# The last normalisation of a diffusion layer: all sums but one tile's by the scalar engine, roots in pairs by GpSimd, both row operations by the vector engine

## The chip, the cores and the metric

The kernel runs on one core of one Trainium2 chip. The metric is the device time of one execution in microseconds (us); of several runs the median counts. The core's engines are TensorE (PE in the profile's rows; PEld are its weight loads), VectorE (DVE), ScalarE (ACT), GpSimd (POOL) and SyncE (SP), which here issues most of the DMAs. Each engine works through its own instructions in order, and semaphores order the engines among each other.

## The reference, cut to what matters

The layer mixes 2048 tokens of 1024 features by neighbourhood attention and a bidirectional mLSTM, sends them through a two-level mixture of experts, and closes with a layer norm. The change touches that last line alone:

```python
def _layer_norm(x, gain=None, bias=None):
    x32 = x.astype(jnp.float32)
    mu = jnp.mean(x32, axis=-1, keepdims=True)
    var = jnp.mean(jnp.square(x32 - mu), axis=-1, keepdims=True)
    y = (x32 - mu) * lax.rsqrt(var + LN_EPS)
    if gain is not None:
        y = y * gain.astype(jnp.float32) + bias.astype(jnp.float32)
    return y.astype(x.dtype)
...
        x_next = _layer_norm(DEEPNORM_ALPHA * x_mid + g2 * moe, ln2_g[l], ln2_b[l])
```

All values are float32. The sum `DEEPNORM_ALPHA * x_mid + g2 * moe` is in the DRAM tensor `acc_d` when the last stage begins: the expert loop adds its outputs there by scattering DMAs.

## The kernel before, in words

The program runs its stages one after the other: modulation, input projection, attention and mLSTM, output projection and first norm, routing, then a loop over expert blocks (L1991 on), whose matmuls read weights that SyncE loads ahead, and whose results GpSimd scatters into `acc_d` (L2048). At the loop's end all engines meet. What follows is the last normalisation (L2094 to L2152), the only part that the change touches.

The 2048 rows are 16 tiles of 128 rows x 1024 columns (0.5 MB each), every one with a buffer of its own (`yy`, 16 buffers), so no load waits for a buffer. SyncE issues the loads of all tiles in order; between them stand two loads of the gain row (after tile 1) and the bias row (after tile 3), spread over 128 partitions (L2105, L2107). A tile goes through four steps: `moments`, `scales`, `gain`, `shifted`. The loop at the end issues `moments` of tile t, `scales` of tile t - 1, `gain` of t - 2 and `shifted` of t - 3 in one turn, and `in_order` keeps each engine's instructions in just the order in which the code names them, so this loop sets the order of every engine's queue.

Which engine does a step is a letter for each tile in the string `WAY`, "ADBADBCDCDBADBAD":

- The sums. In ways B and D (10 tiles) ScalarE makes two passes over the tile, a Copy scaled by -1/1024 whose accumulator gives minus the mean (L2116) and a Square with that as bias whose accumulator gives the sum of squared differences (L2117); the passes' own output goes to a tile `junk` that nobody reads. In A and C (6 tiles) VectorE makes two statistics and an aggregate (L2121, L2122). Two numbers per row result, in the small tile `mvf`.
- The roots. GpSimd makes variance + eps (L2127) and the power -1/2 (L2128) of one column, into `rsf`.
- The row operations. In A and D (10 tiles) VectorE does both, in place: (y - mean) * gain (L2137) and y * root + bias (L2144). In B and C (6 tiles) GpSimd makes a third small number, mean times root (L2131), ScalarE normalises the tile (L2132), GpSimd multiplies by the gain (L2139) and VectorE adds the bias (L2146).

SyncE writes each finished tile to the output (L2147), in the order of tiles.

Of the kernel before, what the change touches and what calls it, by code (L numbers as in the profile page):

```python
# [11 lines left out]
F32 = mybir.dt.float32  # L12
# [4 lines left out]
AF = mybir.ActivationFunctionType  # L17
OP = mybir.AluOpType
# [4 lines left out]
P = 128  # L23
D = 1024
# [4 lines left out]
EPS = 1e-5  # L29
# [6 lines left out]
def tile_layer(ctx, tc, A, out):  # L36
    nc = tc.nc

    def in_order(i):
        return tc.keep_in_program_order(i)  # L40
# [6 lines left out]
    nh = const.tile([P, 4], F32, name="nh")  # L47
# [24 lines left out]
    C = [None, None]  # L72
# [16 lines left out]
    st, ml = {}, {}  # L89
# [22 lines left out]
    with ExitStack() as es, ExitStack() as zes:  # L112
        xg = es.enter_context(tc.tile_pool(name="ip_xg", bufs=1, reuse_waits="tile"))
        ep = es.enter_context(tc.tile_pool(name="ip_e", bufs=4, reuse_waits="tile"))
        cp = es.enter_context(tc.tile_pool(name="ip_c", bufs=1, reuse_waits="tile"))
# [379 lines left out]
        for half in range(2):  # L495
# [94 lines left out]
            for qk in range(2):  # L590
# [5 lines left out]
                for h in range(4):  # L596
# [3 lines left out]
                    for g, n, t0 in groups:  # L600
# [20 lines left out]
                        if gate_rows_:  # L621
                            f, a = gate_rows_.pop(0)
# [261 lines left out]
    junk = []  # L884
# [23 lines left out]
    with ExitStack() as es:  # L908
        kpB = es.enter_context(tc.tile_pool(name="na_kB", bufs=1, reuse_waits="tile"))
        kps.append(kpB)  # L910
        sp = es.enter_context(tc.tile_pool(name="na_s", bufs=3, reuse_waits="tile"))
# [4 lines left out]
        sbs, pTs, pos_, rss, outs = {}, {}, {}, {}, {}  # L916
# [202 lines left out]
    with ExitStack() as es:  # L1119
        cc = es.enter_context(tc.tile_pool(name="op_cc", bufs=2, reuse_waits="tile"))  # L1120
        xn = es.enter_context(tc.tile_pool(name="op_n", bufs=3, reuse_waits="tile"))
        sp = es.enter_context(tc.tile_pool(name="op_s", bufs=4, reuse_waits="tile"))
        cp = es.enter_context(tc.tile_pool(name="op_c", bufs=1, reuse_waits="tile"))
# [608 lines left out]
    with ExitStack() as es:  # L1732
        sp = es.enter_context(tc.tile_pool(name="ro_s", bufs=1, reuse_waits="tile"))
# [4 lines left out]
        for l, G, c0 in ((0, 2, 0), (1, 4, 512)):  # L1738
            n = P // G
# [209 lines left out]
    with ExitStack() as es:  # L1949
        sp = es.enter_context(tc.tile_pool(name="mo_s", bufs=1, reuse_waits="tile"))  # L1950
# [143 lines left out]
    with ExitStack() as es:  # L2094
        cp = es.enter_context(tc.tile_pool(name="fi_c", bufs=1, reuse_waits="tile"))
        yp = es.enter_context(tc.tile_pool(name="fi_y", bufs=16, reuse_waits="tile"))
        sp = es.enter_context(tc.tile_pool(name="fi_s", bufs=4, reuse_waits="tile"))
        nh = cp.tile([P, 1], F32, name="nh2")
        in_order(nc.gpsimd.memset(nh[:], -0.5))
        ln2 = [cp.tile([P, D], F32, name=f"ln2{i}") for i in range(2)]  # L2100
        junk = cp.tile([P, D], F32, name="junk")
        ys, ms, rss = [], {}, {}
        for t in range(16):
            ys.append(yp.tile([P, D], F32, name="yy"))
            in_order(nc.sync.dma_start(ys[t][:], acc_d[t * P : (t + 1) * P, :]))  # L2105
            if t in (1, 3):
                in_order(nc.sync.dma_start(ln2[t // 2][:], A[("ln2_g", "ln2_b")[t // 2]].to_broadcast([P, D])))  # L2107


        WAY = "ADBADBCDCDBADBAD"  # L2110

        def moments(t):
            a = ys[t]
            mv = ms[t] = sp.tile([P, 2], F32, name="mvf")
            if WAY[t] in "BD":
                in_order(nc.scalar.activation(junk[:], a[:], AF.Copy, scale=-1.0 / D, accum_out=mv[:, 0:1]))  # L2116
                in_order(nc.scalar.activation(junk[:], a[:], AF.Square, bias=mv[:, 0:1], accum_out=mv[:, 1:2]))  # L2117
            else:
                st = sp.tile([P, 2, 6], F32, name="stf")
                for hh in range(2):  # L2120
                    in_order(nc.vector.bn_stats(st[:, hh, :], a[:, hh * 512 : (hh + 1) * 512]))  # L2121
                in_order(nc.vector.bn_aggr(mv[:], st[:]))  # L2122

        def scales(t):
            mv = ms[t]
            rs = rss[t] = sp.tile([P, 2], F32, name="rsf")
            in_order(nc.gpsimd.tensor_scalar(rs[:, 0:1], mv[:, 1:2], 1.0 / D if WAY[t] in "BD" else 1.0, EPS, OP.mult, OP.add))  # L2127
            in_order(nc.gpsimd.tensor_tensor(rs[:, 0:1], rs[:, 0:1], nh[:], OP.pow))  # L2128
            if WAY[t] in "AD":
                return  # L2130
            in_order(nc.gpsimd.tensor_scalar(rs[:, 1:2], mv[:, 0:1], rs[:, 0:1], -1.0 if WAY[t] == "C" else 1.0, OP.mult, OP.mult))  # L2131
            in_order(nc.scalar.activation(ys[t][:], ys[t][:], AF.Identity, bias=rs[:, 1:2], scale=rs[:, 0:1]))  # L2132

        def gain(t):
            y = ys[t][:]
            if WAY[t] in "AD":
                in_order(nc.vector.scalar_tensor_tensor(y, y, ms[t][:, 0:1], ln2[0][:], OP.add if WAY[t] == "D" else OP.subtract, OP.mult))  # L2137
            else:
                in_order(nc.gpsimd.tensor_tensor(y, y, ln2[0][:], OP.mult))  # L2139

        def shifted(t):
            y = ys[t][:]
            if WAY[t] in "AD":
                in_order(nc.vector.scalar_tensor_tensor(y, y, rss[t][:, 0:1], ln2[1][:], OP.mult, OP.add))  # L2144
            else:
                in_order(nc.vector.tensor_tensor(y, y, ln2[1][:], OP.add))  # L2146
            in_order(nc.sync.dma_start(out[0, t * P : (t + 1) * P, :], y))  # L2147

        for t in range(16 + 4):
            for f, n in ((moments, t), (scales, t - 1), (gain, t - 2), (shifted, t - 3)):  # L2150
                if 0 <= n < 16:
                    f(n)  # L2152


def consts():
# [62 lines left out]
```

## Time and profile before

| what | value |
|---|---|
| median of 3 runs | 2741.04 us (2736.18 to 2742.62) |
| the profiled execution's own time | 2737.7 us |
| its span, first to last record | 2735.9 us |
| busy share of the span: TensorE, VectorE, ScalarE, GpSimd | 91%, 46%, 29%, 29% |
| last normalisation, first load's issue to the span's end | 2667.30 to 2735.9 us |

The profile is one execution, with all times in us from the span's start. Durations in "mean ns" are nanoseconds. A busy share is an average over stages of different kinds; the change lies in the last 69 us, so the views below are of that stretch. An engine's row in a timeline shows its start, its duration, the instruction, and in brackets how long the engine had been idle before and who ended that. Where a row has "x2", two instructions of one kind that follow each other are merged and the duration is of both. A name such as `yy` stands for all buffers of that name.

### The profile page before, as it was taken

To read this page: it belongs to the slowest core of one execution; us is meant where nothing else is said; L and a number is where in the kernel's file an instruction comes from. 1 tells how busy PE (TensorE), PEld (TensorE's weight loads), DVE (VectorE), ACT (ScalarE), POOL (GpSimd) and SP (SyncE) were. 2 spreads that over 40 slices of the span, in tenths; PEclk is the share of its full clock that TensorE was granted. 3 is DMA by queue.
4 is the path that set the end of the run, shared out by engine and by line. 5 is a ranking of instruction groups with operands and counts; after the bars stand their busy time and mean duration, and the time that the engine had idled before them with its cause. 6 is when DMAs were issued, how large, how long until landed. Compare 5 with 4: busy or idle time off the path is not lost. (4 is left out here: it accounts for less than half of the span.)

```text
span 2735.9 us, 51840 instructions
## 1 busy us (share of the span) xinstructions
PE 2478.8 (91%) x17292; PEld 1567.5 (57%) x17292; DVE 1263.4 (46%) x2891; ACT 799.4 (29%) x1693; POOL 784.5 (29%) x912
## 2 busy tenths in 40 slices
PE   8999999999996899988999589978999999989880
PEld 4778667877886778876887433333333333333330
DVE  5546324357236976656578932222222222222225
ACT  4423115243234666656565410000000000000004
POOL 1212211002034535546434422211222222222127
PEclk9999999999999999999999789989999999999995
DMA  8634762434359979894654689999598897998916
GB/s 267 178 100 133 253 215 89 148 98 153 105 152 252 264 196 216 209 221 134 166 162 135 231 320 369 368 382 346 154 313 308 312 314 235 365 319 312 391 20 261
DMA packets 286892, 626.99 MB, mean 229 GB/s; under 512 B 79448, under 2 KB 142924, under 8 KB 262444
## 3 DMA queue, kind: packets, MB, share of 16 engines
q1 hardware_dynamic: 254716, 564.87, 62.0%
q0 software_dynamic: 31696, 60.09, 9.5%
q8 instruction: 71, 1.16, 0.2%
q10 hardware_dynamic: 352, 0.39, 0.1%
q14 instruction: 57, 0.47, 0.1%
HBM read 947.01 MB, written 97.42 MB: 382 GB/s over the span
## 5 line engine op out<-in xcount | busy, mean ns | idle before, releaser
L2048 POOL DMA_INDIRECT acc_d<-y,ids x112 | 174.4, 1557 | 739.3 <-DMA acc_d<-y,ids 266.4
L2011 DVE TENSOR_TENSOR sg<-sg,ph 128x128 f32<-128x128 f32 x112 | 39.8, 355 | 441.5 <-ACT sg L2010 441.5
L2010 ACT ACTIVATE sg<-ph 128x128 f32<-128x128 f32 x112 | 37.1, 331 | 697.8 <-PE ph L2005 498.1
L2005 PE MATMUL ph<-qkk,xT 128*64 128x512 f32 (+1 forms) x1344 | 234.0, 525 | 3.1 <-DMA qkk<-in_w_dram 3.1
L2005 PE MATMUL ph<-mask,xT 128*64 128x512 f32 x896 | 211.6, 615 | 24.8 <-DMA mask<-in_w_dram 24.8
L246 PE MATMUL ps<-xhi,whi 128*128 128x512 f32 (+1 forms) x576 | 221.6, 386 | 1.6 <-DVE ev L509 1.6
L248 PE MATMUL ps<-xhi,wlo 128*128 128x512 f32 (+1 forms) x576 | 220.2, 382 | 0.5 <-DVE wlo L235 0.5
L247 PE MATMUL ps<-xlo,whi 128*128 128x512 f32 (+1 forms) x576 | 220.3, 382 | 0.0
L2037 PE MATMUL py<-mo,gT 128*64 128x512 f32 x672 | 165.4, 628 | 24.2 <-DMA mask<-in_w_dram 13.2
L255 PE MATMUL ps<-whi,xhi 128*128 128x512 f32 x416 | 166.1, 401 | 1.3 <-ACT whi L234 1.3
L256 PE MATMUL ps<-wlo,xhi 128*128 128x512 f32 x416 | 164.3, 396 | 3.3 <-DVE wlo L235 3.3
L257 PE MATMUL ps<-whi,xlo 128*128 128x512 f32 x416 | 164.8, 397 | 0.0
L960 DVE CUSTOM_DVE_ANT_0 sb<-ps,bias 128x640 f32<-128x640 f32 (+1 forms) x128 | 113.9, 890 | 101.7 <-PE ps L957 78.3
L2005 PEld LDWEIGHTS ph<-mask,xT 128*64 128x64 f32 x896 | 62.1, 140 | 148.0 <-issue 148.0
L2005 PEld LDWEIGHTS ph<-qkk,xT 128*64 128x64 f32 (+1 forms) x1344 | 74.8, 128 | 114.9 <-issue 99.2
L2021 DVE COPY gT<-pg 128x128 f32<-128x128 f32 x112 | 40.2, 359 | 215.4 <-PE pg L2019 215.4
L1972 DVE TENSOR_SCALAR xT<-pxt,mod 128x96 f32<-128x96 f32 x456 | 135.0, 369 | 2.4 <-PE pxt L1965 2.4
L246 PEld LDWEIGHTS ps<-xhi,whi 128*128 128x128 f32 x576 | 108.4, 188 | 28.3 <-issue 3.2
L2045 DVE SCALAR_TENSOR_TENSOR y<-py,wgt,g2r 128x256 f32<-128x256 f32 x112 | 68.7, 613 | 119.5 <-PE py L2037 119.5
L968 ACT ACTIVATE sb<-sb,nm 128x640 f32<-128x640 f32 (+1 forms) x128 | 113.2, 884 | 33.0 <-DVE nm L960 28.8
L2010 ACT ACT_TABLE_LOAD x28 | 35.9, 1283 | 295.0 <-PE ph L2005 295.0
L248 PEld LDWEIGHTS ps<-xhi,wlo 128*128 128x128 f32 x576 | 108.4, 188 | 23.6 <-DVE wlo L235 0.9
(553 smaller groups left out, 5096.2 us busy)
## 6 DMA issues: line engine op xcount, KB each, us to landing
w<-in_w_dram SPq DMA_DIRECT2D x203, 1024.0 KB, 7.6
mask<-in_w_dram SPq DMA_DIRECT2D x114, 1024.0 KB, 8.7
qkk<-in_w_dram SPq DMA_DIRECT2D x114, 1024.0 KB
mo<-in_w_dram SPq DMA_DIRECT2D x171, 512.0 KB, 4.2
bias<-in_w_dram SPq DMA_DIRECT2D x58, 1024.0 KB
xo<-in_w_dram SPq DMA_DIRECT2D x115, 512.0 KB, 9.3
bias<-in_w_dram SPq DMA_DIRECT2D x58, 512.0 KB
qkk<-in_w_dram SPq DMA_DIRECT2D x58, 512.0 KB
```

The costliest lines, as they stand in the source:

```text
L246: nc.tensor.matmul(ps, wh_, xhi[g, k][:], start=k == 0, stop=False)
L247: nc.tensor.matmul(ps, wh_, xlo[g, k][:], start=False, stop=False)
L248: nc.tensor.matmul(ps, wl_, xhi[g, k][:], start=False, stop=k == KC - 1)
L255: nc.tensor.matmul(ps, xh, his[k], start=k == 0, stop=False)
L256: nc.tensor.matmul(ps, xh, los[k], start=False, stop=False)
L257: nc.tensor.matmul(ps, xl, his[k], start=False, stop=k == KC - 1)
L960: in_order(nc.vector.tensor_tensor_reduce(out=sb[:, 0:L], in0=ps[:, off:768], in1=bt[:, 0:L], scale=-0.125, scalar=3.0e38, op0=OP.add, op1 ...
L968: in_order(nc.scalar.activation(sb[:, 0:L], sb[:, 0:L], AF.Exp, bias=nm[:], scale=-1.0, accum_out=rss[n // 8][:, n % 8 : n % 8 + 1]))
L1972: i = nc.vector.tensor_scalar(xT[u][:, k], pxt[:, k, 0:96], mod2[:, 1, k : k + 1], mod2[:, 0, k : k + 1], OP.mult, OP.add)
L2005: in_order(nc.tensor.matmul(ph[j * n : (j + 1) * n], xT[u][:, k, t0 : t0 + n], w13[k][:, :, j * NH : (j + 1) * NH], start=k == 0, stop=k = ...
L2037: in_order(nc.tensor.matmul(py[j * n : (j + 1) * n, :], gT[:, b_, j_ * n : (j_ + 1) * n], w2t[c][:, j * NY : (j + 1) * NY], start=c == 0, ...
L2048: sc = nc.gpsimd.indirect_dma_start(out=acc_d[:].rearrange("t (g n) -> (t g) n", g=G), out_offset=bass.IndirectOffsetOnAxis(ap=ids[u][:, l ...
```

## The change

The table of ways goes. Tile 0 keeps its statistics on VectorE; the sums of the other 15 tiles are ScalarE's two passes. The sums and roots stand in small tiles of two columns, one for each of the pairs (1, 2), (3, 4) to (13, 14), and of one column for tiles 0 and 15; GpSimd makes eps and power for both tiles of a pair in one instruction each, when the second tile's sums are there. Both row operations of all 16 tiles are VectorE's. The gain row is loaded after tile 0 and the bias row after tile 1. All sums and roots are issued first, and then the row operations, the gain of tile t with the shift of tile t - 2.

```diff
@@ -2094,62 +2094,64 @@
     with ExitStack() as es:
         cp = es.enter_context(tc.tile_pool(name="fi_c", bufs=1, reuse_waits="tile"))
         yp = es.enter_context(tc.tile_pool(name="fi_y", bufs=16, reuse_waits="tile"))
-        sp = es.enter_context(tc.tile_pool(name="fi_s", bufs=4, reuse_waits="tile"))
-        nh = cp.tile([P, 1], F32, name="nh2")
+        nh = cp.tile([P, 2], F32, name="nh2")
         in_order(nc.gpsimd.memset(nh[:], -0.5))
         ln2 = [cp.tile([P, D], F32, name=f"ln2{i}") for i in range(2)]
         junk = cp.tile([P, D], F32, name="junk")
-        ys, ms, rss = [], {}, {}
+        ys = []
         for t in range(16):
             ys.append(yp.tile([P, D], F32, name="yy"))
             in_order(nc.sync.dma_start(ys[t][:], acc_d[t * P : (t + 1) * P, :]))
-            if t in (1, 3):
-                in_order(nc.sync.dma_start(ln2[t // 2][:], A[("ln2_g", "ln2_b")[t // 2]].to_broadcast([P, D])))
-
-
-        WAY = "ADBADBCDCDBADBAD"
+            if t < 2:
+                in_order(nc.sync.dma_start(ln2[t][:], A[("ln2_g", "ln2_b")[t]].to_broadcast([P, D])))
+
+
+        pairs_ = [(0, 1), *((t, 2) for t in range(1, 15, 2)), (15, 1)]
+        mvs, rss, at = {}, {}, {}
+        for t0, n in pairs_:
+            mvs[t0] = cp.tile([P, 2, n], F32, name=f"mvf{t0}")
+            rss[t0] = cp.tile([P, n], F32, name=f"rsf{t0}")
+            at.update((t0 + i, (t0, i)) for i in range(n))
 
         def moments(t):
+
             a = ys[t]
-            mv = ms[t] = sp.tile([P, 2], F32, name="mvf")
-            if WAY[t] in "BD":
-                in_order(nc.scalar.activation(junk[:], a[:], AF.Copy, scale=-1.0 / D, accum_out=mv[:, 0:1]))
-                in_order(nc.scalar.activation(junk[:], a[:], AF.Square, bias=mv[:, 0:1], accum_out=mv[:, 1:2]))
-            else:
-                st = sp.tile([P, 2, 6], F32, name="stf")
+            t0, i = at[t]
+            mv = mvs[t0]
+            if t == 0:
+                st = cp.tile([P, 2, 6], F32, name="stf")
                 for hh in range(2):
                     in_order(nc.vector.bn_stats(st[:, hh, :], a[:, hh * 512 : (hh + 1) * 512]))
-                in_order(nc.vector.bn_aggr(mv[:], st[:]))
-
-        def scales(t):
-            mv = ms[t]
-            rs = rss[t] = sp.tile([P, 2], F32, name="rsf")
-            in_order(nc.gpsimd.tensor_scalar(rs[:, 0:1], mv[:, 1:2], 1.0 / D if WAY[t] in "BD" else 1.0, EPS, OP.mult, OP.add))
-            in_order(nc.gpsimd.tensor_tensor(rs[:, 0:1], rs[:, 0:1], nh[:], OP.pow))
-            if WAY[t] in "AD":
+                in_order(nc.vector.bn_aggr(mv[:, :, 0], st[:]))
                 return
-            in_order(nc.gpsimd.tensor_scalar(rs[:, 1:2], mv[:, 0:1], rs[:, 0:1], -1.0 if WAY[t] == "C" else 1.0, OP.mult, OP.mult))
-            in_order(nc.scalar.activation(ys[t][:], ys[t][:], AF.Identity, bias=rs[:, 1:2], scale=rs[:, 0:1]))
+            in_order(nc.scalar.activation(junk[:], a[:], AF.Copy, scale=-1.0 / D, accum_out=mv[:, 0, i : i + 1]))
+            in_order(nc.scalar.activation(junk[:], a[:], AF.Square, bias=mv[:, 0, i : i + 1], accum_out=mv[:, 1, i : i + 1]))
+
+        def roots(t0, n):
+            rs = rss[t0]
+            in_order(nc.gpsimd.tensor_scalar(rs[:], mvs[t0][:, 1, :], 1.0 / D if t0 else 1.0, EPS, OP.mult, OP.add))
+            in_order(nc.gpsimd.tensor_tensor(rs[:], rs[:], nh[:, 0:n], OP.pow))
 
         def gain(t):
-            y = ys[t][:]
-            if WAY[t] in "AD":
-                in_order(nc.vector.scalar_tensor_tensor(y, y, ms[t][:, 0:1], ln2[0][:], OP.add if WAY[t] == "D" else OP.subtract, OP.mult))
-            else:
-                in_order(nc.gpsimd.tensor_tensor(y, y, ln2[0][:], OP.mult))
+            t0, i = at[t]
+            in_order(nc.vector.scalar_tensor_tensor(
+                ys[t][:], ys[t][:], mvs[t0][:, 0, i : i + 1], ln2[0][:], OP.add if t else OP.subtract, OP.mult
+            ))
 
         def shifted(t):
-            y = ys[t][:]
-            if WAY[t] in "AD":
-                in_order(nc.vector.scalar_tensor_tensor(y, y, rss[t][:, 0:1], ln2[1][:], OP.mult, OP.add))
-            else:
-                in_order(nc.vector.tensor_tensor(y, y, ln2[1][:], OP.add))
-            in_order(nc.sync.dma_start(out[0, t * P : (t + 1) * P, :], y))
-
-        for t in range(16 + 4):
-            for f, n in ((moments, t), (scales, t - 1), (gain, t - 2), (shifted, t - 3)):
-                if 0 <= n < 16:
-                    f(n)
+            t0, i = at[t]
+            in_order(nc.vector.scalar_tensor_tensor(ys[t][:], ys[t][:], rss[t0][:, i : i + 1], ln2[1][:], OP.mult, OP.add))
+            in_order(nc.sync.dma_start(out[0, t * P : (t + 1) * P, :], ys[t][:]))
+
+        for t in range(16):
+            moments(t)
+            if t in (0, 15) or t % 2 == 0:
+                roots(t if t in (0, 15) else t - 1, 1 if t in (0, 15) else 2)
+        for t in range(16 + 2):
+            if t < 16:
+                gain(t)
+            if t >= 2:
+                shifted(t - 2)
 
 
 def consts():
```

How the program's instructions stand on SyncE at the start of the stage; `yy` are the tiles, the two `ln` the rows of gain and bias, and - marks before, + after:

```order
-L2105 DMA yy<-acc_d 128x1024 x2
-L2107 DMA ln_15408<-in_ln_g_dram 128x1024
-L2105 DMA yy<-acc_d 128x1024 x2
-L2107 DMA ln_15409<-in_ln_b_dram 128x1024
-L2105 DMA yy<-acc_d 128x1024 x12
+L2104 DMA yy<-acc_d 128x1024
+L2106 DMA ln_15405<-in_ln_g_dram 128x1024
+L2104 DMA yy<-acc_d 128x1024
+L2106 DMA ln_15406<-in_ln_b_dram 128x1024
+L2104 DMA yy<-acc_d 128x1024 x14
```

Tile 1 moves from second to third place, tile 2 from fourth to fifth, tile 3 from fifth to sixth; later tiles keep theirs.

On VectorE the last eight instructions before were these; `yy_15435` to `yy_15443` are tiles 11 to 15, `ln20` the gain, `ln21` the bias:

```order
L2137 SCALAR_TENSOR_TENSOR yy_15437<-yy_15437,mvf_15562,ln20_15408 128x1024
L2144 SCALAR_TENSOR_TENSOR yy_15435<-yy_15435,rsf_15565,ln21_15409 128x1024
L2144 SCALAR_TENSOR_TENSOR yy_15437<-yy_15437,rsf_15574,ln21_15409 128x1024
L2137 SCALAR_TENSOR_TENSOR yy_15441<-yy_15441,mvf_15580,ln20_15408 128x1024
L2146 TENSOR_TENSOR yy_15439<-yy_15439,ln21_15409 128x1024
L2137 SCALAR_TENSOR_TENSOR yy_15443<-yy_15443,mvf_15593,ln20_15408 128x1024
L2144 SCALAR_TENSOR_TENSOR yy_15441<-yy_15441,rsf_15596,ln21_15409 128x1024
L2144 SCALAR_TENSOR_TENSOR yy_15443<-yy_15443,rsf_15602,ln21_15409 128x1024
```

And these are the last eight now; `yy_15432` to `yy_15440` are tiles 11 to 15, and a small tile `mvf13` holds the sums of tiles 13 and 14, `rsf13` their roots:

```order
L2137 SCALAR_TENSOR_TENSOR yy_15436<-yy_15436,mvf13_15456,ln20_15405 128x1024
L2143 SCALAR_TENSOR_TENSOR yy_15432<-yy_15432,rsf11_15455,ln21_15406 128x1024
L2137 SCALAR_TENSOR_TENSOR yy_15438<-yy_15438,mvf13_15456,ln20_15405 128x1024
L2143 SCALAR_TENSOR_TENSOR yy_15434<-yy_15434,rsf11_15455,ln21_15406 128x1024
L2137 SCALAR_TENSOR_TENSOR yy_15440<-yy_15440,mvf15_15458,ln20_15405 128x1024
L2143 SCALAR_TENSOR_TENSOR yy_15436<-yy_15436,rsf13_15457,ln21_15406 128x1024
L2143 SCALAR_TENSOR_TENSOR yy_15438<-yy_15438,rsf13_15457,ln21_15406 128x1024
L2143 SCALAR_TENSOR_TENSOR yy_15440<-yy_15440,rsf15_15459,ln21_15406 128x1024
```

Behind the gain of the last tile stood two shifts, of tiles 14 and 15; now there are three, of tiles 13, 14 and 15. The addition of the bias for a tile that came from GpSimd (L2146) is gone.

## Rows read from the trace of the kernel before

**Rows 1.** The page's part 1: busy us (share of the span) x instructions.
```profile
PE 2478.8 (91%) x17292; PEld 1567.5 (57%) x17292; DVE 1263.4 (46%) x2891; ACT 799.4 (29%) x1693; POOL 784.5 (29%) x912
```

**Rows 2.** Chain that ended last, 2560 to 2736 us: start, duration, what.
```profile
...
2697.80 2.31 POOL yy L2139
...
2723.07 2.32 POOL yy L2139
...
```

**Rows 3.** Waits, 2662 to 2736 us: who waited for whom: us in total, times, longest.
```profile
ACT yy L2132 <- POOL rsf L2131: 20.9, 5, 6.8
DVE yy L2146 <- POOL yy L2139: 15.3, 6, 3.9
...
```

**Rows 4.** Groups of instructions, 2667 to 2736 us: busy us, mean ns | idle before.
```profile
...
L2139 POOL TENSOR_TENSOR yy<-yy,ln 128x1024 f32<-128x1024 f32 x6 | 15.2, 2530 | 0.9 <-ACT yy L2132 0.9
...
```

**Rows 5.** Stretches: length, each engine's busy us, granted clock, DMA share, GB/s.
```profile
2667.00:2731.00 64.00, 0.00 (x0) 0.00 (x0) 39.94 (x44) 31.86 (x47) 48.34 (x45) 0.50 0.68 270
...
2730.00:2732.00 2.00, 0.00 (x0) 0.00 (x0) 0.23 (x1) 0.00 (x0) 0.00 (x0) 0.50 1.00 408
...
```

**Rows 6.** SyncE's timeline, 2667 to 2736 us: start, duration, issue.
```profile
2667.30 0.82 SPq L2105 DMA_DIRECT2D yy<-acc_d  x2
...
2670.36 13.32 SPq L2105 DMA_DIRECT2D yy<-acc_d  x12
...
```

**Rows 7.** VectorE's timeline, 2667 to 2736 us.
```profile
...
2670.96 1.29 DVE L2121 BATCH_NORM_STATS2 stf<-yy 128x6 f32<-128x512 f32 x2 [11.07 <-DMA yy<-acc_d]
...
2674.03 1.28 DVE L2137 SCALAR_TENSOR_TENSOR yy<-yy,mvf,ln 128x1024 f32<-128x1024 f32 x1 [1.54 <-DMA ln<-in_ln_g_dram]
2677.01 1.29 DVE L2121 BATCH_NORM_STATS2 stf<-yy 128x6 f32<-128x512 f32 x2 [1.69 <-DMA yy<-acc_d]
...
2679.71 2.48 DVE L2144 SCALAR_TENSOR_TENSOR yy<-yy,rsf,ln 128x1024 f32<-128x1024 f32 x2
2682.11 1.27 DVE L2137 SCALAR_TENSOR_TENSOR yy<-yy,mvf,ln 128x1024 f32<-128x1024 f32 x1
...
2689.37 2.48 DVE L2144 SCALAR_TENSOR_TENSOR yy<-yy,rsf,ln 128x1024 f32<-128x1024 f32 x2
...
2727.75 2.48 DVE L2144 SCALAR_TENSOR_TENSOR yy<-yy,rsf,ln 128x1024 f32<-128x1024 f32 x2
```

**Rows 8.** ScalarE's timeline, 2667 to 2736 us.
```profile
...
2672.20 1.06 ACT L2116 ACTIVATE junk<-yy 128x1024 f32<-128x1024 f32 x1 [3.62 <-DMA yy<-acc_d]
...
2675.34 1.06 ACT L2116 ACTIVATE junk<-yy 128x1024 f32<-128x1024 f32 x1 [0.72 <-DMA yy<-acc_d]
...
2681.11 1.04 ACT L2116 ACTIVATE junk<-yy 128x1024 f32<-128x1024 f32 x1
...
2683.33 0.19 ACT L2117 ACTIVATION_READ_ACCUMULATOR junk<-yy,mvf 128x1 f32 x1
2683.55 1.06 ACT L2116 ACTIVATE junk<-yy 128x1024 f32<-128x1024 f32 x1
...
```

**Rows 9.** Instructions on the tiles rsf: duration in ns, shortest/median/longest; first and last start.
```profile
L2127 POOL TENSOR_SCALAR rsf<-mvf x16: 192/1042/1227, 2672.7 to 2725.5; 128x1 f32<-128x1 f32 x16
L2128 POOL TENSOR_TENSOR rsf<-rsf,nh x16: 549/568/1567, 2673.0 to 2726.8; 128x1 f32<-128x1 f32 x16
...
L2131 POOL TENSOR_SCALAR rsf<-mvf,rsf x6: 267/926/1932, 2678.8 to 2719.3; 128x1 f32<-128x1 f32 x6
...
```

**Rows 10.** GpSimd's timeline, 2630 to 2736 us.
```profile
...
2672.68 0.19 POOL L2127 TENSOR_SCALAR rsf<-mvf 128x1 f32<-128x1 f32 x1 [5.27 <-DVE mvf L2122]
...
2689.67 1.04 POOL L2127 TENSOR_SCALAR rsf<-mvf 128x1 f32<-128x1 f32 x1
2690.79 1.47 POOL L2128 TENSOR_TENSOR rsf<-rsf,nh 128x1 f32<-128x1 f32 x1
...
```

**Rows 11.** Instructions on the tiles yy, columns as in rows 9.
```profile
...
L2137 DVE SCALAR_TENSOR_TENSOR yy<-yy,mvf,ln x10: 1239/1279/1285, 2674.0 to 2726.6; 128x1024 f32<-128x1024 f32 x10
...
L2144 DVE SCALAR_TENSOR_TENSOR yy<-yy,rsf,ln x10: 1271/1280/1286, 2679.7 to 2728.9; 128x1024 f32<-128x1024 f32 x10
...
```

## Prediction, made before the changed kernel ran

> **What bounds the kernel now.** I read the share of engines on the page first, to place the change: TensorE is busy 91% of the span [rows 1], but the last normalisation comes after its last matmul (TensorE has no instruction in the stage's 64 us [rows 5]), so what a step there costs on the chain of waits is paid in full. Then the chain of waits backwards from the end. It shows, from 2677.78 to 2726.56 us, mostly GpSimd: its full-width multiplies and its root instructions, one behind the other, with a few passes of ScalarE between; the last multiply ends in 2725.4 [rows 2]. The view of waits says the same from the other side: ScalarE sat 20.9 us before its normalising pass for GpSimd's third small instruction, and VectorE 15.3 us before its addition for GpSimd's multiply [rows 3]. The six multiplies alone are 15.2 us, 2.53 us each [rows 4]. In the 64 us from the first load to the last write's issue, VectorE is busy 39.9, ScalarE 31.9, GpSimd 48.3 [rows 5]: no engine is full; three engines take turns on a tile.
>
> The stage has three parts: loads until data flows, a long middle, and a fixed end. SyncE issues the first load at 2667.30 and the last by 2683.68 [rows 6]; tile 0 is there at 2670.96, where VectorE's wait for it ends [rows 7]. VectorE's last instruction begins its pair at 2727.75 and ends at 2730.23 [rows 7]. From there to the span's end (2735.9 us) are 5.67 us: issue of the last write, the write (408 GB/s until 2732 [rows 5]) and what closes the program.
>
> **The change, step by step.** GpSimd loses its six multiplies (15.2 us) and its six third small instructions, ScalarE loses the six normalising passes, VectorE loses five of six statistics and all six additions. GpSimd keeps 18 small root instructions instead of 38. ScalarE now makes 15 pairs of sum passes, VectorE 32 row operations. I ask for each engine what pace it can hold.
>
> *ScalarE.* One tile's two passes, one behind the other, begin at 2681.11 and the next tile's at 2683.55 [rows 8]: 2.44 us a tile, waits for its own accumulator and the DMA wait included. 15 tiles are 36.6 us. They never wait for another engine in the new order, only for loads.
>
> *VectorE.* Two scalar_tensor_tensor from 2679.71 are followed by a third at 2682.11 [rows 7]: 1.20 us from start to start in a row, 2.40 us for the two row operations of a tile. That is 0.04 less than ScalarE needs, so VectorE follows ScalarE tile by tile and waits a little for each.
>
> *Loads.* The gain row now stands second and the bias row fourth in SyncE's queue, so tile 1 is third and tile 2 fifth. What lands third and fifth is in the trace: third landed the gain row (VectorE's wait ended at 2674.03) and fifth tile 3 (2677.01) [rows 7]; ScalarE's waits for tile 1, then second, ended at 2672.20 and for tile 2, fourth, at 2675.34 [rows 8]. So ScalarE does tile 1 at 2674.03 to 2676.47, waits for tile 2 until 2677.01, and then runs through: landings come about 1.5 us apart (four from 2670.96 to 2677.01), faster than 2.44. This is a loss at the front against the old order (about 1.7 us for tile 1).
>
> *The sum.* Tile 15's passes begin at 2677.01 + 13 x 2.44 = 2708.73 and end 2.41 later (2681.11 to 2683.52, the end of the accumulator's read [rows 8]): 2711.14. VectorE wakes about 0.08 later (an estimate: the gap between two GpSimd instructions of which the second needs the first, 2690.71 to 2690.79 [rows 10]) and has four instructions left: the gain of tile 15, the shifts of 13, 14 and 15. Three starts of 1.20 and one whole one of 1.28: 2711.22 + 3.60 + 1.28 = 2716.10, against 2730.23 before: 14.1 us earlier. At the end three writes of 0.5 MB now come 1.20 us apart instead of two; at 408 GB/s one takes 1.28 us, so the last is 0.1 us later still. The fixed end stays 5.67 us. Sum: 14.0 us less, a span of 2721.9.
>
> *Where I cost an edit at nothing: the roots.* A pair's two root instructions must be done when VectorE comes to the first shift of the pair, 2.44 + 0.08 + 1.20 = 3.72 us after the pair's sums. Alone they take 0.19 and about 0.55 us (the shortest of 16 each) [rows 9], but VectorE will be running almost without a gap, and with it they grow: the first up to 1.23, the second up to 1.57 [rows 9]. One case shows how: the instruction that started at 2689.67 ended at 2690.71, and the one at 2690.79 ended at 2692.26 [rows 10], while two row operations ran from 2689.37, the first until about 2690.65 and the second until 2691.85 [rows 7]. Each waited out the row operation then running. 1.23 + 0.08 + 1.57 = 2.88 us is under 3.72; even with the longest small instruction (1.93) in the first's place, 3.58. So the roots stay covered, by 0.14 to 0.84 us. A root of two columns isn't in the trace: it costs from nothing more to as much again as one of one column (0.19 + 0.55 = 0.74); I take nothing, as the one-column instructions differ by what they wait for and not by what they do, and with the 0.74 it is 3.62, still under 3.72. If the cover goes, VectorE stands for what is missing once in each pair. The same holds for tile 15's own root: due 3.68 us after its sums.
>
> Two costs the old trace doesn't show as they will be. VectorE's pace with a wait ahead of each instruction: from below 2.40, from above two separate instructions of 1.28 (their median [rows 11]), 2.56 a tile, which over 15 tiles is 0.12 x 15 = 1.8 us more. I take 2.40, the nearest row: the three from 2679.71 had semaphores of GpSimd and of loads to pass too. The front: at best ScalarE starts at 2672.20 and never waits, 2672.20 + 36.6 = 2708.8, 2.4 us less. So the forecast's own bounds are 16.4 and 12.2 us less.
>
> The profiled execution took 2737.7 us and the runs shown have a median of 2741.04 (2736.18 to 2742.62): 14.0 off the first is 2723.7, off the median 2727.0. The latter is the forecast, since it is against the median of runs that a time will stand.
>
> **The rivals.**
>
> *GpSimd holds VectorE up.* If a root instruction holds up a row operation as the row operations hold up roots, the two root instructions take 0.74 us out of VectorE's time in every pair: 4.80 + 0.74 = 5.54 against ScalarE's 4.88, 0.66 us by 7 pairs = 4.6 us; gain 9.4, time 2731.6. Against it: all 20 row operations took between 1.239 and 1.286 us though root instructions lay beside many [rows 11]. A later start would not show there, so it isn't excluded. The Trainium skill, in "SBUF — State Buffer", section "Who interferes with whom", says that a VectorE instruction with two SBUF inputs and a GpSimd instruction that reads SBUF exclude one another for the whole instruction, whichever starts first. By that rule this rival would hold; the trace agrees for GpSimd's side (0.55 against 1.47 us) and shows no stretched instruction for VectorE's.
>
> *GpSimd starves.* If it gets in only when VectorE stands, VectorE has to stop about 0.08 + 0.19 + 0.08 + 0.55 + 0.08 = 1.0 us in each pair: 5.80 against 4.88, 0.92 x 7 = 6.4; gain 7.6, time 2733.4. For it: one small instruction outlasted a row operation's end and took 1.93 us [rows 9]. Against: the two followed above ended with the row operation beside them or 0.41 us behind it [rows 7, 10].
>
> *Slower: VectorE and GpSimd in turns, with long roots.* If the roots start only when VectorE has stopped and still take their longest, 1.93 + 0.07 + 1.57 = 3.57 us, a pair costs 4.80 + 3.57 = 8.37, 3.49 more than ScalarE's, 24.4 us in 7 pairs: 10.4 us slower, 2751.4. The gain is gone at 2.08 us of standing per pair, and it is slower by the bound below from 3.25. Against: the long times were measured with VectorE running; when it stands they are short (0.19 us for the one that began at 2672.68 [rows 10]).
>
> *The pairs wait for one another.* Both tiles' sums stand in one small tile; should the gain of the first wait for the second's sums, VectorE has eight row operations left at the sums of tile 14 (gains of 13 to 15, shifts of 11 to 15): 8 x 1.20 - 2.44 = 7.2 behind the last sum in place of 4.8; gain 11.6, 2729.4. That would be a change that doesn't quite do what it says.
>
> **How the numbers follow.** Forecast 0.76, GpSimd holds 0.10, starves 0.08, slower 0.03, pairs wait 0.03. The bound for "no change" is 0.3%, 8.2 us, about what a measurement of this kernel can tell. Of the forecast 0.74 lies beyond it and 0.02 within; of the first rival 0.06 and 0.04 (its 9.4 is near the bound); of the second 0.01 and 0.07; the last is beyond, the third slower. Faster 0.84, same 0.13, slower 0.03. The range: below, 2737.7 - 16.4 = 2721.3 and 1.5 less, as the fastest run stood under the profiled one, some 2719; above, the starving case with the highest run's 1.6 over the median, 2735.
>
> **What would show it.** ScalarE's passes without a gap from tile 2 on, tiles starting 2.44 us apart, the last ending near 2711; VectorE busy about 40 us, waits of under 0.1 us for ScalarE and none for GpSimd; root instructions of 1.0 to 1.6 us, beside row operations of 1.28. VectorE's last end at 2716 +- 1.5 and 5.7 us behind it. Wrong would be: waits of VectorE for the roots (second and third rival); starts of row operations more than 1.25 us apart without a wait (first); sums over 2.5 us a tile; or a front where tile 2 lands after 2678.

## The result, and the profile after

The changed kernel's median was 2719.67 us (4 runs, 2719.43 to 2725.97) against 2741.78 before (4 runs, 2736.18 to 2742.62): ratio 0.9928, 95% interval 0.9909 to 0.9946. With more runs on one chip it was 2727.8 (8 runs) against 2741.12 (24 runs), 0.9949, 0.9932 to 0.9967. The forecast was 2727.0, 0.9949 of 2741.04.

The profiled execution's span went from 2735.9 to 2717.9 us, 18.0 less, where 14.0 were forecast. SyncE's timeline of the changed kernel shows where the other 4 us are:

```profile
2663.39 0.35 SPq L2104 DMA_DIRECT2D yy<-acc_d  x1
...
2665.22 14.39 SPq L2104 DMA_DIRECT2D yy<-acc_d  x14
```

The last normalisation begins at 2663.39 and not at 2667.30 [rows 6], 3.9 us earlier, before any changed instruction has run. The stage itself, from its first load's issue to the span's end, took 68.6 us and takes 54.5: 14.1 less. I therefore count all below from the stage's start.

ScalarE's timeline: the waits for tile 1 (third to land) and tile 2 (fifth), the pace, and the end.

```profile
2669.77 1.06 ACT L2127 ACTIVATE junk<-yy 128x1024 f32<-128x1024 f32 x1 [5.10 <-DMA yy<-acc_d]
...
2672.88 1.06 ACT L2127 ACTIVATE junk<-yy 128x1024 f32<-128x1024 f32 x1 [0.69 <-DMA yy<-acc_d]
...
2675.33 1.06 ACT L2127 ACTIVATE junk<-yy 128x1024 f32<-128x1024 f32 x1
...
2704.78 1.06 ACT L2127 ACTIVATE junk<-yy 128x1024 f32<-128x1024 f32 x1
...
2707.02 0.19 ACT L2128 ACTIVATION_READ_ACCUMULATOR junk<-yy,mvf 128x1 f32 x1
```

From tile 2 to tile 15 the starts are (2704.78 - 2672.88) / 13 = 2.454 us apart, without one wait, where rows 8 showed 2.44. VectorE's timeline, the first three gains, two turns of the middle, and the end:

```profile
2668.67 1.29 DVE L2137 SCALAR_TENSOR_TENSOR yy<-yy,mvf,ln 128x1024 f32<-128x1024 f32 x1
2672.22 1.29 DVE L2137 SCALAR_TENSOR_TENSOR yy<-yy,mvf,ln 128x1024 f32<-128x1024 f32 x1 [2.26 <-ACT junk L2128]
2675.33 1.28 DVE L2137 SCALAR_TENSOR_TENSOR yy<-yy,mvf,ln 128x1024 f32<-128x1024 f32 x1 [1.83 <-ACT junk L2128]
2676.54 1.28 DVE L2143 SCALAR_TENSOR_TENSOR yy<-yy,rsf,ln 128x1024 f32<-128x1024 f32 x1
2677.79 1.29 DVE L2137 SCALAR_TENSOR_TENSOR yy<-yy,mvf,ln 128x1024 f32<-128x1024 f32 x1
...
2707.24 1.29 DVE L2137 SCALAR_TENSOR_TENSOR yy<-yy,mvf,ln 128x1024 f32<-128x1024 f32 x1
2708.44 3.67 DVE L2143 SCALAR_TENSOR_TENSOR yy<-yy,rsf,ln 128x1024 f32<-128x1024 f32 x3
```

Starts alternate between 1.20 us (gain to shift) and 1.25 us (shift to the next gain): the 0.05 is VectorE waiting for ScalarE. The three shifts behind the last gain end at 2712.11, 5.79 us ahead of the span's end (5.67 before). In rows 7 VectorE's instructions stood between waits for other engines; now there is one row operation after another.

GpSimd's timeline, the first pair's roots, and all instructions on the small tiles (ns, shortest/median/longest), which answer to rows 10 and 9:

```profile
2675.39 1.28 POOL L2132 TENSOR_SCALAR rsf<-mvf 128x2 f32<-128x2 f32 x1 [4.72 <-ACT junk L2128]
2676.76 1.62 POOL L2133 TENSOR_TENSOR rsf<-rsf,nh 128x2 f32<-128x2 f32 x1
```

```profile
L2143 DVE SCALAR_TENSOR_TENSOR yy<-yy,rsf,ln x16: 1279/1280/1281, 2676.5 to 2710.8; 128x1024 f32<-128x1024 f32 x16
L2132 POOL TENSOR_SCALAR rsf<-mvf x9: 677/1283/1285, 2668.7 to 2707.9; 128x2 f32<-128x2 f32 x7, 128x1 f32<-128x1 f32 x2
L2133 POOL TENSOR_TENSOR rsf<-rsf,nh x9: 582/1609/1623, 2670.1 to 2708.7; 128x2 f32<-128x2 f32 x7, 128x1 f32<-128x1 f32 x2
```

The first root instruction begins 0.06 us after the gain from 2675.33 and ends (2676.67) 0.06 after it. The second begins in the shift from 2676.54 and ends (2678.38) 0.56 after that one's end (2677.82). And the waits, against the 20.9 and 15.3 us of rows 3:

```profile
POOL rsf L2132 <- ACT junk L2128: 16.3, 7, 4.7
...
ACT junk L2127 <- DMA yy<-acc_d: 5.8, 2, 5.1
...
DVE yy L2137 <- ACT junk L2128: 4.1, 2, 2.3
```

No engine waits for GpSimd any more; GpSimd waits for ScalarE. The stretch from the first load to VectorE's end is 49 us and no longer 64. The row has each engine's busy us (columns as in rows 5); VectorE's 40.74 are about as many as before (39.94), GpSimd's 24.38 half of its 48.34:

```profile
2663.00:2712.00 49.00, 0.00 (x0) 0.00 (x0) 40.74 (x35) 37.14 (x61) 24.38 (x19) 0.50 0.87 344
```

### The profile page after: what moved, and what is told of

Its sections match the earlier page's. It is cut to its first block, busy times and chain, and to the rows that moved or that the text cites. A ratio compares the mean times of both kernels' runs of the same rounds, so it can differ in the third digit from the quotient of the medians.

```text
span 2717.9 us, 51820 instructions
## 1 busy us (share of the span) xinstructions
PE 2481.7 (91%) x17292; PEld 1568.7 (58%) x17292; DVE 1268.3 (47%) x2882; ACT 804.9 (30%) x1707; POOL 759.1 (28%) x886
## 5 line engine op out<-in xcount | busy, mean ns | idle before, releaser
L247 PEld LDWEIGHTS ps<-xlo,whi 128*128 128x128 f32 x576 | 108.3, 188 | 23.0 <-DVE xlo L182 0.9
```

The lines of the kernel that those rows point to most:

```text
L247: nc.tensor.matmul(ps, wh_, xlo[g, k][:], start=False, stop=False)
```

## The experiments

My theory (A): the stage gained 14.1 us as worked out, ScalarE's sums setting the pace and the roots covered; what the times show beyond that is the spread of the earlier stages from execution to execution. The rival (B): the change also makes the earlier, unchanged stages faster, by where code and buffers lie. Within the stage the rivals of the prediction stand: GpSimd's roots hold VectorE up, or set the pace. For all runs, from the timelines (us after the stage's start; "sums" is the end of ScalarE's last accumulator read, "VectorE" the end of its last row operation):

| kernel | stage starts | sums | VectorE | stage |
|---|---|---|---|---|
| before | 2667.30 | 57.5 | 62.9 | 68.6 |
| before_again | 2676.05 | 57.9 | 63.3 | 69.2 |
| forecast | | 43.8 | 48.8 | 54.6 |
| after | 2663.39 | 43.8 | 48.7 | 54.5 |
| after_again | 2674.30 | 43.9 | 48.8 | 54.5 |
| ways_only | 2660.66 | 43.2 | 47.4 | 53.2 |
| old_loads | 2672.44 | 42.8 | 47.7 | 53.6 |
| third_root | 2671.72 | 43.9 | 50.0 | 55.8 |
| no_roots | 2666.87 | 43.8 | 48.8 | 54.8 |
| lean | 2668.72 | 42.9 | 47.1 | 52.8 |

**Both kernels again, unedited (before_again, after_again).**

> The kernel before, unchanged, against itself: how far one kernel's executions lie apart, and where in the program. Theory A (the stage gained 14.1 us, as forecast, and what the times show beyond that is spread of the earlier stages between executions): this profile's last stage, from its first load's issue to the span's end, is 68.6 us within 0.5 as in the first trace, but the stage starts anywhere between 2662 and 2670 us; the runs spread over 4 to 7 us. Theory B (the change also makes the earlier stages some 4 us faster, by where code and buffers lie): the stage starts at 2667 within 1 here, and at 2663.5 within 1 in every kernel with the new end.

> The changed kernel, unchanged, with more runs. Theory A: last stage 54.5 us within 0.5, its start anywhere between 2662 and 2670; over many runs the gain is 14 to 18 us, so the ratio's interval reaches 0.9945. Theory B: the stage starts at 2663.5 within 1 and the gain stays at 18 to 22 us, ratio 0.992 to 0.9935.

Measured: 11 runs of the kernel before lay between 2732.08 and 2747.79 us, with 1.0002 (0.9988 to 1.0016) against its other runs. 8 runs of the changed kernel lay between 2716.99 and 2730.78, ratio 0.9949. The first load of the stage, in SyncE's timeline of before_again and then of after_again:

```profile
2676.05 0.83 SPq L2105 DMA_DIRECT2D yy<-acc_d  x2
```

```profile
2674.30 0.35 SPq L2104 DMA_DIRECT2D yy<-acc_d  x1
```

The same kernel starts the stage at 2667.30 and at 2676.05, the changed one at 2663.39 and at 2674.30; over all nine profiles it is 2660.66 to 2676.05, and of these nine starts the old kernel's two are the fourth and the last. The stage's length stays within 0.7 us for one kernel. So B as I put it falls: its 2663.5 within 1 was missed by 10.8, and the ratio 0.9949 lies above the 0.992 to 0.9935 that it asked for (though the interval begins at 0.9932). An effect of a few us on the earlier stages would not show in two profiles of a kernel and isn't excluded. The spread was wider than A expected (11 runs spread over 15.7 us instead of 4 to 7, starts of the stage beyond 2662 and 2670), and the stage of before_again was 69.25, 0.15 outside its bounds.

Over half of the difference between two executions of one kernel is there before the expert loop. The 16 writes to `acc_d` that come before that loop (L1245), in before, before_again, after and after_again:

```profile
L1245 SPq DMA_DIRECT2D acc_d<-xa x16: 517/558/1554, 1321.6 to 1560.3; - x16
L1245 SPq DMA_DIRECT2D acc_d<-xa x16: 517/559/1726, 1327.4 to 1565.9; - x16
L1245 SPq DMA_DIRECT2D acc_d<-xa x16: 517/559/1822, 1320.3 to 1559.6; - x16
L1245 SPq DMA_DIRECT2D acc_d<-xa x16: 517/558/565, 1325.5 to 1565.3; - x16
```

The last of them starts 5.6 us apart in the one kernel (of 8.75 at the stage's start) and 5.7 apart in the other (of 10.9).

**One string of the old kernel (ways_only).** Old order of issue, roots tile by tile, old loads; only who does what is the new kernel's.

```diff
-        WAY = "ADBADBCDCDBADBAD"
+        WAY = "ADDDDDDDDDDDDDDD"
```

> The kernel before with one string changed: tile 0 by way A, the other 15 by way D. So the engines' work is that of the changed kernel, but roots are made tile by tile, the shift of tile t - 1 follows the gain of tile t, and the loads keep their old order. Theory C (ScalarE's 2.45 us a tile sets the pace, roots stay covered also one by one): tile 2 is in its sums 1.5 us earlier than in the changed kernel and two instructions instead of three follow the last gain, so the last stage takes 51.5 to 52.5 us. Theory D (root instructions wait out a row operation each, 1.28 + 0.08 + 1.61 = 2.97 us a tile, and this is more than 2.45, so GpSimd sets the pace): 7 to 8 us longer than the changed kernel's stage, 59 to 62 us.

Measured: stage 53.2 us, 2721.7 us median (9 runs), ratio 0.9942 (0.9925 to 0.9958). The work of the engines alone, without pairs, without the new order of loads and issue, brings the whole gain and 1.3 us more of the stage. C's mechanism holds but its size was 0.7 off; D (59 to 62) falls. ScalarE's timeline, tile 2 and tile 15; VectorE's, the wait for the bias row, two row operations of the middle and the end; GpSimd's two instructions of one tile:

```profile
2668.88 1.06 ACT L2116 ACTIVATE junk<-yy 128x1024 f32<-128x1024 f32 x1 [0.95 <-DMA yy<-acc_d]
...
2701.43 1.06 ACT L2116 ACTIVATE junk<-yy 128x1024 f32<-128x1024 f32 x1
...
2703.67 0.19 ACT L2117 ACTIVATION_READ_ACCUMULATOR junk<-yy,mvf 128x1 f32 x1
```

```profile
2671.48 1.28 DVE L2144 SCALAR_TENSOR_TENSOR yy<-yy,rsf,ln 128x1024 f32<-128x1024 f32 x1 [1.42 <-DMA ln<-in_ln_b_dram]
...
2696.59 1.28 DVE L2137 SCALAR_TENSOR_TENSOR yy<-yy,mvf,ln 128x1024 f32<-128x1024 f32 x1
2697.79 1.28 DVE L2144 SCALAR_TENSOR_TENSOR yy<-yy,rsf,ln 128x1024 f32<-128x1024 f32 x1
...
2702.58 1.28 DVE L2144 SCALAR_TENSOR_TENSOR yy<-yy,rsf,ln 128x1024 f32<-128x1024 f32 x1
2703.89 1.28 DVE L2137 SCALAR_TENSOR_TENSOR yy<-yy,mvf,ln 128x1024 f32<-128x1024 f32 x1
...
2706.81 1.28 DVE L2144 SCALAR_TENSOR_TENSOR yy<-yy,rsf,ln 128x1024 f32<-128x1024 f32 x1 [0.44 <-POOL rsf L2128]
```

```profile
2679.23 0.75 POOL L2127 TENSOR_SCALAR rsf<-mvf 128x1 f32<-128x1 f32 x1
2680.07 1.47 POOL L2128 TENSOR_TENSOR rsf<-rsf,nh 128x1 f32<-128x1 f32 x1
```

VectorE began late, as it waited 1.42 us for the bias row, and then ran without a gap, 1.20 us from start to start, until it had caught up with ScalarE: the last sums end at 2703.86 and the last gain begins at 2703.89. So ScalarE's sums set the end here too, as C had it. They were (2701.43 - 2668.88) / 13 = 2.50 us apart and not 2.45, which is 0.65 us over 13 tiles, and VectorE stood 0.44 us for the last root: together 1.1 of the 1.2 us by which the stage lies over the middle of C's band (52.0).

GpSimd's instructions for the next tile begin at 2681.62, 2.39 after these. Each got in at the end of the row operation then running, so two of them cost GpSimd two row operations, which is just what VectorE needs for a tile: GpSimd runs in step, not behind. D had the first of the two wait out a whole row operation (1.28 us); here it came in the middle of one and took 0.75.

**The old places of gain and bias row (old_loads).**

```diff
-            if t < 2:
+            if t in (1, 3):
-                in_order(nc.sync.dma_start(ln2[t][:], A[("ln2_g", "ln2_b")[t]].to_broadcast([P, D])))
+                in_order(nc.sync.dma_start(ln2[t // 2][:], A[("ln2_g", "ln2_b")[t // 2]].to_broadcast([P, D])))
```

> The changed kernel with the gain and bias rows loaded after tiles 1 and 3, as before. If the front is what the prediction said (tile 1 and tile 2 land one place later, a loss of 1.7 us), tile 2's sums begin 1.3 to 1.7 us earlier after the stage's start and the stage takes 52.8 to 53.2 us instead of 54.5. If VectorE or GpSimd sets the pace instead, the stage keeps its 54.5.

```profile
2677.59 1.06 ACT L2127 ACTIVATE junk<-yy 128x1024 f32<-128x1024 f32 x1 [3.87 <-DMA yy<-acc_d]
...
2680.90 1.06 ACT L2127 ACTIVATE junk<-yy 128x1024 f32<-128x1024 f32 x1 [0.89 <-DMA yy<-acc_d]
```

ScalarE's timeline: tile 2 begins 2680.90 - 2672.44 = 8.46 us after the stage's start, not 9.49; sums and VectorE end 1.0 earlier, the stage 0.9. The direction is right (the front's loss goes straight through to the end, so ScalarE sets the pace), the size 0.3 to 0.7 under what I expected, and the stage's 53.6 lies 0.4 over its band. Tile 2 in fourth place began its sums at 8.04 in the kernel before [rows 6, 8], 8.11 in before_again, 8.22 in ways_only and 8.46 here. Two executions of one kernel differ by under 0.1, so why it came later here is open.

**A third root instruction (third_root).**

```diff
             in_order(nc.gpsimd.tensor_scalar(rs[:], mvs[t0][:, 1, :], 1.0 / D if t0 else 1.0, EPS, OP.mult, OP.add))
+            if 0 < t0 < 15:
+                in_order(nc.gpsimd.tensor_scalar(rs[:], mvs[t0][:, 1, :], 1.0 / D if t0 else 1.0, EPS, OP.mult, OP.add))
             in_order(nc.gpsimd.tensor_tensor(rs[:], rs[:], nh[:, 0:n], OP.pow))
```

> The changed kernel with the first root instruction of each of the seven pairs made twice, so GpSimd has three small instructions in a row for a pair instead of two. In the changed kernel's trace a pair's roots end 2.98 us after its sums and are due 3.67 after. If roots wait out one row operation each and cover is 0.7 us as so measured, the third wait (1.2 us) breaks it. Theory E (as the prediction put it: VectorE stands once in each pair for what is missing): 0.5 to 0.6 us by seven pairs, the stage 3.5 to 4.2 us longer, 58 to 58.7. Theory F (VectorE stands once, then runs behind ScalarE by that much and the later roots come earlier in its time): 0.4 to 1.3 us longer in all, 54.9 to 55.8. If the roots don't wait for row operations at all: 54.5.

VectorE's three waits for roots (pair 1, 2; pair 13, 14; tile 15), then the first root instruction of the second, third and fourth pair in GpSimd's timeline:

```profile
2688.05 1.28 DVE L2145 SCALAR_TENSOR_TENSOR yy<-yy,rsf,ln 128x1024 f32<-128x1024 f32 x1 [0.60 <-POOL rsf L2135]
...
2717.49 2.48 DVE L2145 SCALAR_TENSOR_TENSOR yy<-yy,rsf,ln 128x1024 f32<-128x1024 f32 x2 [0.58 <-POOL rsf L2135]
2720.42 1.28 DVE L2145 SCALAR_TENSOR_TENSOR yy<-yy,rsf,ln 128x1024 f32<-128x1024 f32 x1 [0.45 <-POOL rsf L2135]
```

```profile
2688.68 0.71 POOL L2132 TENSOR_SCALAR rsf<-mvf 128x2 f32<-128x2 f32 x1 [0.66 <-ACT junk L2128]
...
2693.58 0.59 POOL L2132 TENSOR_SCALAR rsf<-mvf 128x2 f32<-128x2 f32 x1 [1.30 <-ACT junk L2128]
...
2698.49 0.46 POOL L2132 TENSOR_SCALAR rsf<-mvf 128x2 f32<-128x2 f32 x1 [1.43 <-ACT junk L2128]
```

1.3 us longer in all (55.8): F, at its upper end, and not E. VectorE stood 0.60 at the first pair and then ran 0.6 behind ScalarE, so the next pair's sums came in the middle of a row operation and the first root instruction had only its rest to wait out: 0.71, 0.59, 0.46. From pair to pair this rest is 0.12 to 0.13 shorter, since VectorE, at 1.195 from start to start, makes up that much; when it had caught up, at the pair 13, 14, it stood again, and a third time for the last root. That VectorE stands at all shows that the cover is there and small: in the changed kernel's trace the first pair's roots are done at 2678.38 and the shift that needs them begins at 2678.99, 0.6 us later (they end 3.08 us after the sums' end at 2675.30, not the 2.98 that I had read).

**No roots (no_roots).**

```diff
+        for t0, n in pairs_:
+            in_order(nc.gpsimd.memset(rss[t0][:], 1.0))
         for t in range(16):
             moments(t)
-            if t in (0, 15) or t % 2 == 0:
-                roots(t if t in (0, 15) else t - 1, 1 if t in (0, 15) else 2)
```

> The changed kernel without the root instructions: the root tiles are set to 1 at the stage's start, so the output lacks the division by the standard deviation. Rival of the prediction (GpSimd's root instructions hold VectorE's row operations up): starts of row operations move from 1.20 and 1.25 us apart to 1.20 and the stage gets shorter by up to 4.6 us, 50 to 53. Theory A (VectorE isn't held up, ScalarE's sums set the pace): row operations start as before by turns 1.20 and 1.25 apart, stage 54.3 to 54.6.

VectorE's timeline and its row operations' durations (ns):

```profile
2678.84 1.28 DVE L2137 SCALAR_TENSOR_TENSOR yy<-yy,mvf,ln 128x1024 f32<-128x1024 f32 x1 [1.83 <-ACT junk L2128]
2680.04 1.28 DVE L2143 SCALAR_TENSOR_TENSOR yy<-yy,rsf,ln 128x1024 f32<-128x1024 f32 x1
2681.29 1.28 DVE L2137 SCALAR_TENSOR_TENSOR yy<-yy,mvf,ln 128x1024 f32<-128x1024 f32 x1
```

```profile
L2143 DVE SCALAR_TENSOR_TENSOR yy<-yy,rsf,ln x16: 1276/1277/1280, 2680.0 to 2714.3; 128x1024 f32<-128x1024 f32 x16
```

The same 1.20 and 1.25, VectorE's end at 48.8 as with roots (48.7), the shifts 3 ns shorter. The rival that roots hold VectorE up falls: they cost VectorE nothing here. The stage's 54.8 misses my 54.3 to 54.6 by what lies behind VectorE's end, 6.1 us against 5.8.

**A leaner version (lean).** Roots tile by tile, each shift right behind the next gain, rows after tiles 1 and 2.

```diff
-            if t < 2:
+            if t in (1, 2):
-                in_order(nc.sync.dma_start(ln2[t][:], A[("ln2_g", "ln2_b")[t]].to_broadcast([P, D])))
+                in_order(nc.sync.dma_start(ln2[t - 1][:], A[("ln2_g", "ln2_b")[t - 1]].to_broadcast([P, D])))
...
-        pairs_ = [(0, 1), *((t, 2) for t in range(1, 15, 2)), (15, 1)]
+        pairs_ = [(t, 1) for t in range(16)]
...
-            if t in (0, 15) or t % 2 == 0:
-                roots(t if t in (0, 15) else t - 1, 1 if t in (0, 15) else 2)
-        for t in range(16 + 2):
-            if t < 16:
-                gain(t)
-            if t >= 2:
-                shifted(t - 2)
+            roots(t, 1)
+        gain(0)
+        for t in range(16):
+            if t < 15:
+                gain(t + 1)
+            shifted(t)
```

> A version put together from the parts: the changed kernel's small tiles (none used twice), but roots tile by tile, the shift of tile t right behind the gain of tile t + 1 (two row operations instead of three after the last gain), and the rows loaded after tiles 1 and 2. From the trace with one string changed: VectorE ran 1.196 us from start to start and stood 1.4 us for the bias row and 0.4 for the last root. With the bias row one place earlier: VectorE's last end 46.2 to 46.8 us after the stage's start, stage 52.0 to 52.6 us, against 53.2 and 54.5; the time 2 us under the changed kernel's, which is less than the runs can tell (ratio 0.993 to 0.995). If ScalarE still sets the pace: its last sums end at 42.5, and the stage is 52.3 to 53.

Measured: stage 52.8 us, the shortest of all, in the band for ScalarE's pace (52.3 to 53; its sums ended at 42.9, not 42.5) and 0.2 over the other; VectorE's end at 47.1, not 46.2 to 46.8. The time is 2724.97 us (5 runs), ratio 0.9943 (0.993 to 0.9957). It beats both kernels in the stage, by 15.8 and 1.7 us; against the changed kernel the times can't show it. Its last two shifts, VectorE's timeline:

```profile
2712.81 1.28 DVE L2143 SCALAR_TENSOR_TENSOR yy<-yy,rsf,ln 128x1024 f32<-128x1024 f32 x1
2714.53 1.28 DVE L2143 SCALAR_TENSOR_TENSOR yy<-yy,rsf,ln 128x1024 f32<-128x1024 f32 x1 [0.44 <-POOL rsf L2133]
```

With one shift less behind the last gain, part of the last root is no longer covered: VectorE stands 0.44 us for it. Even so both versions without the pairs, ways_only and this one, have a shorter stage than the changed kernel.

## Why the prediction was right, step by step

- **The bound.** Right. Three engines taking turns, most of all around GpSimd's multiplies, were the stage's length; ways_only, which changes only who does what, gives the whole gain. It takes away the multiplies, the third small instructions and the normalising passes and moves five tiles' statistics to ScalarE, all at once; which of these gave how much was not tried apart.
- **ScalarE's pace** was 2.44 and measured 2.454: 0.2 us more over 13 tiles, made up by luck, by tile 2 landing 9.49 us after the stage's start instead of 9.71. End of the sums forecast at 43.84, measured 43.82.
- **VectorE's pace** and the four instructions at the end: forecast 48.80, measured 48.72. The waits of 0.05 a tile were foreseen; the two of 2.26 and 1.83 us at the first gains I had not named, but they follow from the loads.
- **The fixed end** 5.77 forecast, 5.79 measured.
- **The roots' cover.** Right that they are covered and that each that meets a running row operation waits for its end. Mis-sized: a root of two columns cost more, 1.61 us against 1.47 to 1.48 with one column, where I took nothing. Wrong: "VectorE stands for what is missing once in each pair". third_root shows that it stands at the first pair, then runs late by as much, and later roots come in time: 1.3 us in all instead of 3.5 to 4.2. The starving rival and the slower one multiplied a loss by seven too, but for roots that don't get in beside a running row operation at all; third_root says nothing of their prices.
- **The rivals.** GpSimd holds VectorE up: refuted by no_roots. Starves: no wait of VectorE for a root in the changed kernel, and roots ended 0.06 or 0.56 us behind the row operation. Slower: no. The pairs wait: the gain of tile 1 begins at 2672.22, as its sums end (2672.19), and not with tile 2's. Of the rule of the Trainium skill that the prediction cited ("SBUF — State Buffer", "Who interferes with whom"), the runs show GpSimd's side: a root instruction that met a running row operation ended behind that one's end. They show no row operation held up by a root.
- **The time.** 2719.67 lies 7.3 us under the forecast and just inside the range, 0.7 over its lower end. That it lies inside at all was luck: in the profiled execution the stage began 3.9 us earlier than in the one before, for no reason that the forecast names. The step that was too tight is the last one, from the stage's 14.0 us to a median of runs: I let the runs spread by 1.5 us to either side, where 11 runs of one kernel spread over 15.7 us. The larger sample (2727.8, a gain of 13.3) lies near the forecast's 2727.0; its interval, 0.9932 to 0.9967, is a gain of 9 to 19 us. The stage's own 14.1 is the better witness for the forecast's 14.0.

## What to carry to other kernels

When three engines take turns on a tile and none is full, try giving each one a whole kind of work and compare their paces per tile. Here the end was then the start of the second tile's sums, plus ScalarE's pace times the tiles, plus what must still follow the last tile. Leave on an engine that a nearly full one holds up (here GpSimd beside VectorE) only what is small enough to get in between, and ask when it is due. Then try each part of such a change alone: the new split of the work gave the whole gain here, and the pairs and the new order weren't needed for it. A change in one stage of a long program is measured by that stage's own span in the trace, since the unchanged stages ahead of it can differ by more than it brings.

## What the runs showed of the hardware that I had not expected

- The unchanged program ahead of the stage ended anywhere from 2660.66 to 2676.05 us in nine executions, 15 us apart, with the stage itself within 0.7 us for one kernel. In nine profiles the last write ahead of the expert loop (L1245) already started between 1556.3 and 1567.4, 11 us apart. What makes the earlier stages differ was not settled.
- A root instruction of GpSimd that a row operation of VectorE held up got in at that operation's end in every profile, even with the next one following without a gap: it ended 0.04 to 0.07 us (eps), 0.40 to 0.44 (power, one column) or 0.54 to 0.57 (power, two columns) behind it, and VectorE lost nothing. Not every small instruction got in so: in the kernel before, a third one (L2131) that began in the first of two shifts ended 0.04 us behind the second (2721.24 against 2721.20).

```profile
2718.72 2.48 DVE L2144 SCALAR_TENSOR_TENSOR yy<-yy,rsf,ln 128x1024 f32<-128x1024 f32 x2
```

```profile
2719.31 1.93 POOL L2131 TENSOR_SCALAR rsf<-mvf,rsf 128x1 f32<-128x1 f32 x1
```

- Where small tiles were used again by later tiles (ways_only, four buffers), ScalarE's sums were 2.51 us a tile apart (2676.35 to 2678.86), against 2.45 in kernels whose tiles aren't; the longer steps begin with tile 4, the first that uses a buffer again. That the buffers are the cause was not tried, and the kernel before, with the same four, has a step of 2.44 [rows 8].
